# One broadcast for two factors in the feed-forward norm, and 64 more bytes ahead of V0 and V1

## The chip, the cores and the metric

The kernel runs on one core of a Trainium2 chip, in one launch. The time is the device time of one execution in microseconds (us). Beside the timed runs there is one profiled execution, from which all rows of the trace come. Engines are named as in the profile: PE is TensorE (PEld its weight loads), DVE is VectorE, ACT is ScalarE, POOL is GpSimd, SP issues the DMAs of the weights.

## What is computed

A sequence of 256 tokens of width 1024 goes through two layers of a first block and one layer of a second block, all in float32. A layer of the first block is

```
h = h + 0.5 * swiglu(rmsnorm(h, ffn1_norm), ffn1_wg, ffn1_wu, ffn1_wd)
h = h + hybrid_mixer(rmsnorm(h, mix_norm), ...)
h = h + 0.5 * swiglu(rmsnorm(h, ffn2_norm), ffn2_wg, ffn2_wu, ffn2_wd)
gate = sigmoid(rmsnorm(h, ple_norm) @ ple_w_gate);  h = h + gate * (p @ ple_w_proj)

swiglu(x, wg, wu, wd) = (silu(x @ wg) * (x @ wu)) @ wd          # 1024 -> 2816 -> 1024
```

`rmsnorm` divides each token by the root of its mean square plus 1e-6 and multiplies by a gain for each channel. The mixer projects the normed h, runs a short convolution branch and a state space branch (with a grouped norm and the product `m_w_out`, 2048 to 1024), gates and adds them and ends with `w_o`. The second block has a pooling and a convolution branch, and a feed-forward of squared relu, `w_up_2` (1024 to 4096) and `w_down_2`. So there are four gated feed-forwards, and their norm and their factor 0.5 are what the change touches.

## The kernel before, in words

**Layout.** Activations lie with channels on the 128 partitions and the 256 tokens along the free axis. A product with a weight matrix is cut into tiles of 128x128, 4948 in all, which SP loads in pieces of eight, in the order in which they are used. Each piece is split into two float32r parts (lines 319 to 333): ScalarE rounds it to `whi`, VectorE subtracts to `wlo`. The activations are split in the same way into a `hi` and a `lo` half. One tile is then three matmuls of 256 columns (`mm3`, lines 366 to 378): `whi` with hi, `whi` with lo, `wlo` with hi. The weight tile is the stationary operand, the activation the moving one. In the trace the operand's tile gives the name: `bank<-hs,whi` for instance is a product of the activations in hs0 or hs1.

**Where the activations lie.** hs0 and hs1 (lines 213 and 214, 16384 bytes in each partition) take turns as the operand of a stage that reads normed or raw h. The 22 blocks of a feed-forward's inner activations lie in V0 and V1, 11 in each (line 418); the mixer's 16 blocks of normed y lie there as well, as the operand of `m_w_out`. The mixer's merged branches lie in mg, the operand of `w_o`, at the place of the tile X. In the second block's feed-forward blocks 0 to 21 are in V0 and V1 and blocks 22 to 31 in V2, also at the place of X (line 1278). There the roles are exchanged (`mm3_rows`, lines 349 to 364): the activation is the stationary operand and 512 columns of weights the moving one, six matmuls for each of the 32 blocks, in two halves.

The allocator places the tiles one behind the other in the order of the code, with 32 bytes for a `small`. `more`, a tile of 192 bytes (line 516), comes behind X and ahead of ya, V0, V1, xd0 and xd1. In bytes from the start of a partition: weights' raw, whi and wlo tiles from 16512, each 4096 long; hs0 74048; hs1 90432; X (and mg and V2) 142912; more 167488; ya 167680; V0 175872; V1 198400; xd0 220928; xd1 (where p_sp lies) 225024.

**Order.** A small planner, `Flow` (lines 84 to 129), keeps an estimated clock for each engine while the program is written out: every stage is a generator that yields its estimated costs, and the order in which generators wake up is the order of the instructions on each engine. The order of the weight tiles is that of the main generator. [...]

**A feed-forward** (`ffn`, lines 541 to 588). Gate and up are 22 blocks each, with K of 8 tiles, from hs: 2 x 22 x 8 x 3 = 1056 matmuls. They start before the norm is known, since the norm's factor is one number for each token and can be multiplied in afterwards: hs holds h times the channel gains. The norm runs beside them (`norm`, lines 477 to 490): a column sum of the squares (two fp32 matmuls of 128 columns with a matrix of ones into the one PSUM bank `side`, `colsum`), the inverse root by Newton steps on VectorE (`rsqrt`), and then a broadcast (`bcast`, lines 468 to 475): the factors of 128 tokens stand one on each partition, and a matmul with the identity turns them into a row that is the same on all partitions, twice for 256 tokens. In the trace each fp32 matmul of these shows as two, so a broadcast is four rows `side<-ident,small`, and a column sum is four rows `side<-ones,acc`. ScalarE evicts the side bank into a row tile. The feed-forward wants the factor twice: `rb`, which multiplies the gate before its Silu, and `rhb`, half of it, which multiplies the result of the down product. Each gets a broadcast and an eviction of its own, the second with a scale of 0.5. In the first feed-forward of all there is no column sum, since its sums come from a copy of x with tokens on the partitions.

As soon as `rb` is there, each block is finished by `gate` (lines 549 to 560): a multiply on VectorE, Silu on ScalarE, a multiply, and the split into V. Down is 8 blocks with K of 22 tiles from V, 8 x 22 x 3 = 528 matmuls; the first two blocks are done side by side (`heads_of`), so that the last blocks of V have time to arrive.

**Other users of the broadcast.** The mixer's norm and the second block's norms ask for one row each; `norm_y` (lines 778 to 789) makes four broadcasts, one for each group of the grouped norm; the layer norm of the second block one.

Of the kernel before, what the change touches and what calls it, by code (L numbers as in the profile page):

```python
# [9 lines left out]
F32 = mybir.dt.float32  # L10
# [7 lines left out]
P = 128  # L18
T = 256
# [174 lines left out]
class Build:  # L194
# [270 lines left out]
            y = z  # L465
        self.roots.put(lock)

    def bcast(self, row, cols, scale=1.0):

        b = yield from self.side.get()  # L470
        for tt in range(2):
            w = self.mm(b[:, tt * P:(tt + 1) * P], cols[:, tt:tt + 1].to_broadcast([P, P]), self.ident, cost=0.213)
        yield w
        yield self.act(row, b[:, :T], scale=scale)
        self.side.put(b)

    def norm(self, s, rows, ev):

        c, y = self.small[8][:, :2], self.small[9][:, :2]
        yield s["ev"]  # L480
        self.chains += 1
        if "cols" in s:
            c = s["cols"]
        else:
            yield from self.colsum(s, EPS, D, c)
        yield from self.rsqrt(y, c)
        for row, scale in rows:
            yield from self.bcast(row, y, scale)
        self.fire(ev)
        self.chains -= 1  # L490

# [7 lines left out]
    def setup(self):  # L499
        nc = self.nc  # L500
        self.early = a = 32
        nc.sync.dma_start(self.vec[:, :a], self.vecd[:, :a])
        self.xev = [Event() for _ in range(ND)]
        self.flow.use("dma", 1.8)
        make_identity(nc, self.ident)
        nc.vector.memset(self.ones, 1.0)
        nc.vector.memset(self.shim, 0.0)

        nc.vector.memset(self.mask, 0.0)
        nc.gpsimd.affine_select(out=self.mask, in_=self.mask, pattern=[[1, P]], compare_op=ALU.is_ge,  # L510
                                fill=NEG, base=0, channel_multiplier=-1)
        self.chains = 0
        self.started = [Event() for _ in PIECES]
        extra = self.big.tile([P, 6, S * P], F32, name="extra", tag="X")
        self.extra = [extra[:, i, :] for i in range(6)]
        more = self.big.tile([P, 6, 8], F32, name="more", tag="more")
        self.small[18:] = [more[:, i, :] for i in range(6)]
        self.raws.free[:0] = self.extra
        for cv in self.cv.free:
            nc.vector.memset(cv[:, :16], 0.0)  # L520
        self.act(self.small[0], self.ones[:, :8], AF.Silu)
# [68 lines left out]
    def mixer(self, layer, sp, s, next_gain):  # L590
# [5 lines left out]
        rb = yield from self.rows.get()  # L596
# [38 lines left out]
        for n in range(ND):  # L635
            b = bs[1 + n] if n < 3 else (yield from self.unit("w_in", layer, GA + n, sp, ND))
# [141 lines left out]
        def norm_y(ys):  # L778
            for e in gsev:
                yield e  # L780
            yr = self.small[10]
            yield from self.rsqrt(yr, self.gsum)
            for g in range(4):
                gb = yield from self.rows.get()
                yield from self.bcast(gb, yr[:, 2 * g:2 * g + 2])
                row = Shared(self.rows, gb, 4)
                for j in range(4 * g, 4 * g + 4):
                    self.spawn(norm_block(ys, j, row))
                    yield 0.8

        def norm_block(ys, j, row):
            t = yield from self.vv.get()
            yield self.stt(t, xb[:, j, :], self.v("m_norm", layer, j), row.item, ALU.mult, ALU.mult)
            row.put()
            yield from self.split(ys, j, t)
            self.vv.put(t)
# [14 lines left out]
        for g in range(4):  # L811
# [4 lines left out]
            yield from heads(g)  # L816
        ys = Operand(*self.halves())
        self.spawn(norm_y(ys))

        sg = [self.big.tile([P, 4, T], F32, name="sg", tag=("xd0", "xd1")[i]) for i in range(2)]  # L820
# [10 lines left out]
        for n in range(ND):  # L831
            b = yield from self.unit("sc_w_out", layer, n, sc, ND)
            self.spawn(branch_a(n, b))
        for n in range(ND):
            b = yield from inp(GM + n)
# [18 lines left out]
        for n in range(ND):  # L854
            b = yield from self.unit("m_w_out", layer, n, ys, 16)
# [10 lines left out]
        for n in range(ND):  # L866
            b = bs[n] if n < 4 else (yield from self.unit("w_o", layer, n, mg, ND))
# [109 lines left out]
    def second(self, sp, ss):  # L977
# [9 lines left out]
        rb, r1b = (yield from self.rows.get()), (yield from self.rows.get())  # L987
# [3 lines left out]
        def norms():  # L991


            v1, v2, v12, r1, r12 = (x[:, :2] for x in self.small[12:17])
            yield from self.colsum(ss[0], EPS, D, v1)
            yield from self.colsum(ss[1], 0.0, D, v2)
            yield self.stt(v12, v1, EPS, v2)
            yield from self.rsqrt(r12, v12)
            yield from self.bcast(rb, r12)
            self.fire(rev)  # L1000
            for n in range(ND):
                yield from self.idle("dve")
                yield self.stt(xf[:, n, :], self.h[:, n, :], self.v("norm_mix_pre_2", None, n), rb, ALU.mult, ALU.mult)
                self.fire(xfo.ev[n])
            yield from self.rsqrt(r1, v1)
            yield from self.bcast(r1b, r1)
            yield 30.0
            for n in range(0, ND, 2):
                yield from self.idle("dve")
                yield self.mul(self.h[:, n:n + 2, :], self.h[:, n:n + 2, :], r1b.unsqueeze(1).to_broadcast([P, 2, T]))  # L1010
            self.rows.put(r1b)
            self.fire(hev)

        self.spawn(norms())

        def glu_part(n, ba, bg):
# [109 lines left out]
        for n in range(NSPLIT):  # L1126
            b = yield from self.unit(W, 0, 12 + n, sp, ND)
            self.spawn(gate(n, b))
        self.drop(sp)
        for n in range(NSPLIT, 2 * ND):  # L1130
            b = yield from self.unit(W, 0, 12 + n, xfo, ND)
# [6 lines left out]
        def layer_norm():  # L1138
            yield cvdone
            self.chains += 1  # L1140
            b = yield from self.banks.get()
            for n in range(4):
                w = self.mm(b[:, :T], self.ones, cacc[:, n, :], n == 0, n == 3, cost=0.43)
            yield w
            mu = yield from self.rows.get()
            yield self.act(mu, b[:, :T], scale=1.0 / 512)
            self.banks.put(b)
            yield self.sub(cacc, cacc, mu.unsqueeze(1).to_broadcast([P, 4, T]))
            self.rows.put(mu)
            p = yield from pr.get()  # L1150
            yield self.act(p, cacc, AF.Square)
            yield self.add(p[:, 0:2, :], p[:, 0:2, :], p[:, 2:4, :])
            s = yield from self.new_sum(0)
            yield self.add(s["acc"], p[:, 0, :], p[:, 1, :])
            pr.put(p)
            self.fire(s["ev"])
            c, rl = self.small[18][:, :2], self.small[19][:, :2]
            yield from self.colsum(s, EPS, 512, c)
            if sgev[-1].on:
                self.act(self.small[5], self.ones[:, :8], AF.Silu)  # L1160
            yield from self.rsqrt(rl, c)
            rlb = yield from self.rows.get()
            yield from self.bcast(rlb, rl)
            self.chains -= 1
            row = Shared(self.rows, rlb, 4)
            for n in range(4):
                self.spawn(ln_out(n, row))
                yield 0.4

        def ln_out(n, row):  # L1170
            t = yield from self.t.get()
            yield self.mul(t, cacc[:, n, :], row.item)
            row.put()
            yield self.act(t, t, AF.Silu, scale=self.v("conv_ln_g_2", None, n), bias=self.v("conv_ln_b_2", None, n))
            yield from self.split(pc, n, t)
            self.t.put(t)

        self.spawn(layer_norm())

        def mixed(n, b):  # L1180
# [3 lines left out]
        for n in range(4):  # L1184
            b = yield from self.banks.get()
# [11 lines left out]
        for n in range(ND):  # L1197
            b = yield from self.unit("w_pool_out_2", 0, n, px, 4)
# [13 lines left out]
        for n in range(ND):  # L1212
            b = yield from self.unit("w_conv_out_2", 0, n, pc, 4)
# [14 lines left out]
        for n in range(ND):  # L1228
            b = bs[n] if n < 4 else (yield from self.unit("w_o_2", 0, n, mg, ND))
            self.spawn(out(n, b))  # L1230
        self.drop(mg)
        rb = yield from self.rows.get()
# [16 lines left out]
        row = Shared(self.rows, rb, ND)  # L1249
# [29 lines left out]
        for j in range(NF2):  # L1279
            b = bs[j] if j < H else (yield from self.unit("w_up_2", 0, j, nsp, ND))  # L1280
# [6 lines left out]
        row = self.big.tile([P, D], F32, name="gain", tag="xd0")  # L1287
# [158 lines left out]
```

## Time and profile before

| what | value |
|---|---|
| timed runs | 1841.87, 1833.98, 1841.28 us; median 1841.28 |
| profiled execution | 1848.41 us, its span 1846.6 us |
| mean granted TensorE clock | 0.995 |
| matmuls | 14916 |
| DVE, ACT, POOL busy | 1316.8, 1050.3, 10.5 us |
| weights from HBM | 340.31 MB read, 185 GB/s over the span |

How to read the rows below: a group's row gives line, engine, operation, output<-inputs, shape, count, then busy time and the mean duration of one, then the engine's idle time before them. A window's row gives the stretch in us from the span's start, its length, the busy time and count of TensorE, the granted clock, the share of DMA time and GB/s. A row of the timeline begins with its start and length in us. [...]

### The profile page before, as it was taken

Reading aid. Unit: us, or ns where it says so; the run is one execution under the profiler, and the core shown is the slowest. Engines: PE = TensorE matmul, PEld = TensorE weight load, DVE = VectorE, ACT = ScalarE, POOL = GpSimd, SP = SyncE. Lnnn points to the kernel's source line nnn. Section 1 sums busy time; section 2 is a strip of 40 time slices with the busy share of each in tenths; the row PEclk is TensorE's granted clock in tenths of the full one; section 3 lists DMA queues with packets and bytes.
Section 4 is the critical chain, followed back from the end, with each engine's and each line's share of the span. In section 5 each row is a group of like instructions: output and inputs, shape, how many; then the busy total and the mean of one; then the engine's idle time right before and its main releaser. Section 6 shows DMA issues by size and latency. Waiting matters only on the chain.

```text
span 1846.6 us, 36550 instructions
## 1 busy us (share of the span) xinstructions
PE 1817.4 (98%) x14916; PEld 1776.4 (96%) x14916; DVE 1316.8 (71%) x2236; ACT 1050.3 (57%) x1707; POOL 10.5 (1%) x22
## 2 busy tenths in 40 slices
PE   8999999999999999999999999999999999989997
PEld 8999999999999999999999999999999999889986
DVE  6666789888576656866578988766665689877643
ACT  5554678665454444644457966555544468656542
POOL 0000000000000000000000000000000000000000
PEclk9999999999999999999999999999999999989999
DMA  7666576655656665665557666465666653546552
GB/s 253 204 195 186 161 252 194 220 180 158 203 169 196 184 186 179 187 187 186 183 169 255 186 199 191 157 204 189 190 189 184 184 181 126 175 149 204 184 192 76
DMA packets 92696, 343.83 MB, mean 186 GB/s; under 512 B 10448, under 2 KB 10960, under 8 KB 91376
## 3 DMA queue, kind: packets, MB, share of 16 engines
q1 hardware_dynamic: 90720, 327.25, 57.1%
q0 software_dynamic: 1520, 13.73, 2.0%
q8 instruction: 116, 1.90, 0.4%
q10 hardware_dynamic: 288, 0.52, 0.1%
q14 instruction: 52, 0.43, 0.1%
HBM read 340.31 MB, written 1.15 MB: 185 GB/s over the span
## 4 chain that ended last, share of the span: by engine, by line
PE 92%; DVE 3%; ACT 2%; DMA 2%; issue 1%; SPq 0%; DVEq 0%; ACTq 0%
PE bank L237 90%; DMA raw<-in_w 1%; PE side L237 1%; DVE wlo L244 1%; ACT L266 1%; ACT whi L266 1%; PE bank L733 0%; DMA h<-in_x 0%; ACT dec L266 0%; DVE small L257 0%; DVE cv L257 0%; DVE hs L257 0%; DVE acc L244 0%; DVE t L244 0%; DVE vv L257 0%
## 5 line engine op out<-in xcount | busy, mean ns | idle before, releaser
L237 PE MATMUL bank<-hs,whi 128*128 128x256 f32 x6928 | 1224.7, 281 | 12.0 <-ACT whi L266 7.5
L237 PEld LDWEIGHTS bank<-hs,whi 128*128 128x128 f32 x6928 | 1058.0, 189 | 19.2 <-ACT whi L266 7.8
L244 DVE TENSOR_TENSOR wlo<-raw,whi 128x1024 fp32r<-128x1024 f32 (+1 forms) x602 | 732.2, 1219 | 397.7 <-ACT whi L266 396.9
L266 ACT ACTIVATE whi<-raw 128x1024 fp32r<-128x1024 f32 (+1 forms) x602 | 634.5, 1057 | 660.1 <-issue 343.4
L237 PE MATMUL bank<-hs,wlo 128*128 128x256 f32 x3464 | 968.9, 280 | 1.0 <-DVE wlo L244 1.0
L237 PEld LDWEIGHTS bank<-hs,wlo 128*128 128x128 f32 x3464 | 656.6, 190 | 1.8 <-DVE wlo L244 1.7
L237 PE MATMUL bank<-V,whi 128*128 128x256 f32 x1920 | 342.7, 282 | 0.0
L237 PEld LDWEIGHTS bank<-V,whi 128*128 128x128 f32 x1920 | 295.3, 188 | 0.0
L237 PE MATMUL bank<-V,wlo 128*128 128x256 f32 x960 | 270.8, 282 | 0.0
L237 PEld LDWEIGHTS bank<-V,wlo 128*128 128x128 f32 x960 | 180.8, 188 | 0.0
L237 PE MATMUL bank<-whi,V 128*128 128x512 f32 x256 | 80.3, 393 | 0.0
L244 DVE TENSOR_TENSOR t<-bank,row 128x256 f32<-128x256 f32 x159 | 64.2, 416 | 19.4 <-PE bank L237 12.5
L257 DVE SCALAR_TENSOR_TENSOR cv<-bank,vec,cv 128x253 f32<-128x253 f32 (+2 forms) x144 | 63.4, 472 | 2.9 <-ACT cv L266 2.5
L244 DVE TENSOR_TENSOR vv<-bank,t 128x256 f32<-128x256 f32 x152 | 62.5, 417 | 3.1 <-ACT t L266 2.9
L244 DVE TENSOR_TENSOR V<-vv,V 128x256 fp32r<-128x256 f32 x152 | 62.2, 418 | 1.5 <-ACT V L266 1.3
L266 ACT ACTIVATE V<-vv 128x256 fp32r<-128x256 f32 x152 | 59.9, 402 | 2.6 <-DVE vv L257 1.6
L237 PEld LDWEIGHTS bank<-whi,V 128*128 128x128 f32 x256 | 48.2, 188 | 11.1
L237 PE MATMUL bank<-wlo,V 128*128 128x512 f32 x128 | 50.5, 394 | 0.0
L266 ACT ACTIVATE dec<-dec,tb 128x256 f32<-128x256 f32 (+1 forms) x128 | 49.5, 444 | 0.1
L244 DVE TENSOR_TENSOR acc<-acc,sq 128x256 f32<-128x256 f32 x101 | 42.3, 419 | 8.8 <-ACT sq L266 8.2
L266 ACT ACT_TABLE_LOAD x37 | 47.5, 1283 | 1.3 <-PEq L1441 0.7
L237 PE MATMUL bank<-mg,whi 128*128 128x256 f32 x256 | 45.3, 281 | 0.0
(152 smaller groups left out, 1114.7 us busy)
## 6 DMA issues: line engine op xcount, KB each, us to landing
raw<-in_w SPq DMA_DIRECT2D x613, 512.0 KB, 4.3
dec<-cum_d POOLq DMA_DIRECT2D x8, 1536.0 KB, 10.1
extra<-in_w SPq DMA_DIRECT2D x4, 512.0 KB, 8.3
xt<-in_xt SPq DMA_DIRECT2D x1, 1024.0 KB, 11.3
h<-in_x SPq DMA_DIRECT2D x1, 512.0 KB, 8.2
praw<-in_p POOLq DMA_DIRECT2D x2, 256.0 KB, 4.6
gain<-in_row POOLq DMA_DIRECT2D x1, 512.0 KB, 4.8
out<-o SPq DMA_DIRECT2D x2, 256.0 KB, 2.7
```

The costliest lines, as they stand in the source:

```text
L237: self.nc.tensor.matmul(ps, w, x, start=start, stop=stop, **k)
L244: self.nc.vector.tensor_tensor(out, a, b, op=op)
L257: self.nc.vector.scalar_tensor_tensor(out, a, s, b, op0=op0, op1=op1)
L266: self.nc.scalar.activation(out=out, in_=a, func=func, **k)
```

## The change

`bcast` takes a list of rows with their scales. It broadcasts once and evicts the side bank into each of the rows, one eviction behind the other, and gives the bank back after the last. `norm` hands it both rows of the feed-forward at once, so that the second broadcast of each of the four feed-forwards is gone and both evictions read the same bank. The other callers hand over a list of one.

`more` grows from 6 x 8 to 8 x 8 numbers, from 192 to 256 bytes in each partition. The two added entries are not used. Everything behind it lies 64 bytes higher: ya 167744, V0 175936, V1 198464, xd0 220992, xd1 225088. V0 and V1 then start 64 bytes past a multiple of 256, as hs0 does.

```diff
-    def bcast(self, row, cols, scale=1.0):
+    def bcast(self, rows, cols):
 
         b = yield from self.side.get()
         for tt in range(2):
             w = self.mm(b[:, tt * P:(tt + 1) * P], cols[:, tt:tt + 1].to_broadcast([P, P]), self.ident, cost=0.213)
         yield w
-        yield self.act(row, b[:, :T], scale=scale)
+        for row, scale in rows:
+            wait = self.act(row, b[:, :T], scale=scale)
+        yield wait
         self.side.put(b)
...
         yield from self.rsqrt(y, c)
-        for row, scale in rows:
-            yield from self.bcast(row, y, scale)
+        yield from self.bcast(rows, y)
         self.fire(ev)
...
-        more = self.big.tile([P, 6, 8], F32, name="more", tag="more")
+        more = self.big.tile([P, 8, 8], F32, name="more", tag="more")
         self.small[18:] = [more[:, i, :] for i in range(6)]
...
-                yield from self.bcast(gb, yr[:, 2 * g:2 * g + 2])
+                yield from self.bcast([(gb, 1.0)], yr[:, 2 * g:2 * g + 2])
```

More of the change, by code (lines that the diff above doesn't have):

```diff
@@ L998, in norms @@
             yield from self.rsqrt(r12, v12)
-            yield from self.bcast(rb, r12)
+            yield from self.bcast([(rb, 1.0)], r12)
             self.fire(rev)
@@ L1005, in norms @@
             yield from self.rsqrt(r1, v1)
-            yield from self.bcast(r1b, r1)
+            yield from self.bcast([(r1b, 1.0)], r1)
             yield 30.0
@@ L1162, in layer_norm @@
             rlb = yield from self.rows.get()
-            yield from self.bcast(rlb, rl)
+            yield from self.bcast([(rlb, 1.0)], rl)
             self.chains -= 1
```

## The prediction

> **What bounds the kernel now.** I read the page first, for the engine that sets the end, then the groups of matmuls by operand, then windows of TensorE by stage, and at last the order of TensorE's instructions where the feed-forward norm cuts into it.
>
> ```profile
> PE 1817.4 (98%) x14916; PEld 1776.4 (96%) x14916; DVE 1316.8 (71%) x2236; ACT 1050.3 (57%) x1707; POOL 10.5 (1%) x22
> PE 92%; DVE 3%; ACT 2%; DMA 2%; issue 1%; SPq 0%; DVEq 0%; ACTq 0%
> L237 PE MATMUL bank<-V,whi 128*128 128x256 f32 x1920 | 342.7, 282 | 0.0
> L237 PE MATMUL bank<-V,wlo 128*128 128x256 f32 x960 | 270.8, 282 | 0.0
> L237 PE MATMUL bank<-whi,V 128*128 128x512 f32 x256 | 80.3, 393 | 0.0
> ```
>
> TensorE is busy for 98% of the span, and 92% of the chain that ended last is TensorE. The V groups waited for nothing (0.0). So the time is the number of matmuls times the distance from one start to the next, and a change moves the time if it moves that distance. The duration of one (282 ns) is no help: it overlaps its neighbours. The distance comes from windows laid inside one stage: length plus one matmul (0.28 us), divided by the count, since a matmul that only reaches into the window is counted too.
>
> ```profile
> core 0: us, PE busy (x), PEclk, DMA share, GB/s
> 31.40:133.90 102.50, 102.50 (x907) 1.00 0.67 201
> 135.00:195.00 60.00, 60.00 (x508) 1.00 0.64 185
> 197.50:204.50 7.00, 7.00 (x64) 1.00 0.66 199
> 438.90:442.60 3.70, 3.70 (x35) 1.00 0.57 167
> 443.40:447.60 4.20, 4.20 (x38) 1.00 0.29 110
> 453.00:469.00 16.00, 16.00 (x143) 1.00 0.69 221
> 470.00:514.00 44.00, 44.00 (x373) 1.00 0.62 194
> 515.00:536.00 21.00, 21.00 (x180) 1.00 0.50 156
> 537.50:542.80 5.30, 5.30 (x47) 1.00 0.85 294
> 548.80:662.90 114.10, 114.10 (x971) 1.00 0.62 189
> 664.00:725.00 61.00, 61.00 (x516) 1.00 0.63 188
> 768.90:880.20 111.30, 111.30 (x947) 1.00 0.62 190
> 881.00:943.00 62.00, 62.00 (x519) 1.00 0.60 186
> 1297.00:1410.00 113.00, 113.00 (x962) 1.00 0.64 191
> 1412.00:1473.00 61.00, 61.00 (x517) 1.00 0.62 187
> 1745.00:1774.00 29.00, 29.00 (x126) 1.00 0.56 182
> 1776.00:1787.00 11.00, 11.00 (x50) 1.00 0.60 192
> ```
>
> By stage, in ns: gate and up of the first feed-forward (31.4) 113.3; its down, from V, 118.7; the mixer's last product from hs (453) 113.8; m_w_out, from V, (470) 118.7; w_o, from mg, (515) 118.2; gate and up of the second feed-forward (548.8) 117.8, its down 118.8; of the third (768.9) 117.8, its down 120.0; of the fourth 117.8 and 118.5. The granted clock is 1.00 in every row and TensorE has no idle time, so neither clock nor waiting makes the difference. There are three paces. The same tiles hs0 and hs1 run at **A**, 113.3, or **B**, 117.8, for a whole stage; V never runs at either, but at **C**, 118.7 to 120.0.
>
> What goes with C is the place. In the allocation of the kernel before, hs0 and hs1 start 64 bytes past a multiple of 256 in each partition (74048, 90432), mg and V2 too (142912), the weights 128 past one, V0 and V1 0 past one (175872, 198400). The last stage shows the same with V as stationary operand: over V0 and V1 (1745) 233 ns a matmul with the 393 ns of its row for the edge, over V2 (1776) 228.
>
> What chooses A or B is the break. The norm's fp32 broadcasts cut into the stream, and after each the pace can be another:
>
> ```profile
> 28.38 0.28 PE L237 MATMUL bank<-hs,wlo 128*128 128x256 f32 x1
> 28.72 0.28 PE L237 MATMUL bank<-hs,wlo 128*128 128x256 f32 x1
> 28.84 0.60 PE L237 MATMUL side<-ident,small 128*128 128x128 f32 x4
> 29.52 0.28 PE L237 MATMUL bank<-hs,wlo 128*128 128x256 f32 x1
> 29.87 0.28 PE L237 MATMUL bank<-hs,wlo 128*128 128x256 f32 x1
> 30.58 0.28 PE L237 MATMUL bank<-hs,wlo 128*128 128x256 f32 x1
> 30.69 0.61 PE L237 MATMUL side<-ident,small 128*128 128x128 f32 x4
> 31.38 0.28 PE L237 MATMUL bank<-hs,wlo 128*128 128x256 f32 x1
> 31.72 0.28 PE L237 MATMUL bank<-hs,wlo 128*128 128x256 f32 x1
> ...
> 546.84 0.28 PE L237 MATMUL bank<-hs,wlo 128*128 128x256 f32 x1
> 546.96 0.61 PE L237 MATMUL side<-ident,small 128*128 128x128 f32 x4
> 547.32 0.49 PE L237 MATMUL bank<-hs,whi 128*128 128x256 f32 x2
> 547.65 0.28 PE L237 MATMUL bank<-hs,wlo 128*128 128x256 f32 x1
> 547.99 0.28 PE L237 MATMUL bank<-hs,wlo 128*128 128x256 f32 x1
> 548.10 0.65 PE L237 MATMUL side<-ident,small 128*128 128x128 f32 x4
> ```
>
> Three matmuls lie between two wlo starts: 0.34 us is A, 0.35 to 0.36 is B. In the first feed-forward the stream is at A, the first broadcast puts it at B, the second back at A, and there it stays for 907. In the second it comes at B (537.5: 118.7, short), the first broadcast puts it at A (547.65 to 547.99: 0.34), the second at B, and there it stays for 971. The mixer's breaks alternate too: 35 in 3.7 us are A (B would give 34), 38 in 4.2 us are B (A would give 39).
>
> **The change, part by part.** *The second broadcast goes*, once in each of four feed-forwards. From 28.72 to 29.52 are 0.80 us where 0.34 would be without the break: 0.46 each, four times, all on TensorE's path: **-1.8**. The second eviction stays as an instruction and comes right behind the first:
>
> ```profile
> L266 ACT ACTIVATE row<-side x24: 366/385/387, 29.5 to 1648.4; 128x256 f32<-128x256 f32 x24
> ```
>
> Its 0.385 us lie beside the first gate multiply on VectorE, which needs only the first row; behind it on ScalarE is that gate's Silu, which waits for the multiply anyway. Without that cover it costs 4 x 0.39 = 1.5 us, of ScalarE, not TensorE. The side bank comes free one eviction later, and its next user is a whole stage away. No wait is added, and no DMA or queue is passed.
>
> *The pace after the norm turns over.* This is worth more than the instructions. In the first feed-forward, the pace after the first broadcast is now kept: 907 matmuls at B for A, 907 x 4.5 ns = **+4.0**. In the second, third and fourth the row before the removed break is at A (shown for the second; the third and fourth end at B like it, and I take them alike): 971, 947 and some 971 at A for B: -4.3, -4.2, -4.3 = **-12.8**.
>
> *V0 and V1 move 64 bytes*, to hs0's place in 256. The trace has no V there; the nearest rows are hs, between 113.3 and 117.8, and V itself as it is, up to 120.0. I take what the stage before it runs at, since mg goes on into hs at one pace without a break (515 and 537.5). From the code, down has 8 x 22 x 3 = 528 matmuls, m_w_out 8 x 16 x 3 = 384, w_o 192. First down, after B: 528 x 0.9 = **-0.5**, and the first 69 of the mixer behind it, now at A (197.5: 113.8), +**0.3**. Both m_w_out follow A: 768 x 5.3 = **-4.1**. Behind them w_o and the 48 heads of the next gate keep A for B: 480 x 4.4 = **-2.1**. The other downs: 2 x 528 x 5.3 = -5.6, and from 120.0 528 x 6.6 = -3.5: **-9.1**. In the last stage 2 x 22 x 6 = 264 matmuls are nearer V2's pace: 5 ns by the windows, of which I trust 4, **-1.0**. p_sp, 96 matmuls, moves as V does: between 0 and -0.5, taken **-0.3**. Elementwise operands that shift along count nothing: their engines are at 71% and 57%.
>
> The sum: -1.8 + 4.0 - 12.8 - 0.5 + 0.3 - 4.1 - 2.1 - 9.1 - 1.0 - 0.3 = **-27.4 us**. The profiled execution took 1848.41 (span 1846.6), so 1821.0. The runs shown, 1833.98 to 1841.87, lie 6.5 to 14.4 below it, spread by 7.9. I read that as the same choice of pace: the second break comes five matmuls after the first and waits for the eviction (0.65 for 0.61), so its outcome can differ between runs, at 4.3 us a feed-forward. The changed kernel has no such break; so I take off only 1 us: **1820**.
>
> Do the feeding engines keep up with A everywhere? The first gate stage ran at A over 102 us with 201 GB/s and no wait, so I expect no new bound.
>
> [...]
>
> **The rivals.** *The first feed-forward stays at A* (the start, with its waits, leaves the stream so that one break ends at A): -4.0, -0.3, and its down gains 2.8 for 0.5: 1821.0 - 6.6 = 1814. For it: the start differs from every other stage. Against: the rows at 28.72 to 30.58 are B. *The later gates stay at B*, only V gains: 1821.0 + 12.8 = 1834. For it: all three end at B now. Against: 547.65 to 547.99. *The place does nothing*, and the paces stay as they are: 1848.4 - 1.8 = 1846.6, which beside the runs is no change. For it: C could belong to the work beside it, such as the down stage's evictions. Against: m_w_out has other work beside it and the same 118.7. [...] *Slower: B is carried on.* Once the first feed-forward ends at B and V no longer interrupts it, B runs into the mixer and through its breaks. It decides at the first break after 204.5. +4.0, V at B for C 2880 x 0.9 and 0.7 more for the 120.0 stage (-3.3), -1.8, -1.0, and the mixers' hs products, 2 x 1920 by the code and about half at A now: 1920 x 4.4 = +8.4, all of them +16.9. That is +6.3 to +14.8, 1855 to 1863, 1859 in the middle. Against: both mixer rows (438.9, 443.4) show breaks that turn B to A.
>
> **How the numbers follow.** The forecast has 0.50, the first feed-forward at A 0.17, later gates at B 0.12, no effect of place 0.15, B carried on 0.06. About 0.5%, 9 us, is what can be told from no change: against a median of 1841, faster is below 1832. The first two cases are, and most of the third against the profiled time: 0.78; same 0.16; slower 0.06. The range goes down to 1808 (the second case less the 6 us by which runs lie under the profile) and up to 1836 (the third, with the mixers' breaks 2 us either way).
>
> **What would show it.** Windows over the changed trace: first gates near 117.8, the other three near 113.3; downs at 113 to 118, none at 118.7; w_o at 113.3; the last stage even over its 32 steps. One broadcast before each gate stage with two evictions behind it. V at 118.7 again makes the place wrong; gates at 117.8 make the break wrong; TensorE waits in the gates would mean that the feeding engines don't keep up.

## The result and the profile after

The changed kernel takes 1820.8 us (median of four, 1818.1 to 1822.13), the kernel before 1841.57 beside it (1833.98 to 1847.4): a ratio of 0.9888, 95% interval 0.9849 to 0.9926. The profiled execution took 1822.13, its span 1820.3, which is 26.3 us less than the span before. The medians differ by less, 20.8, since the profiled execution before (1848.41) lies above all the timed runs beside it; what differs between executions of that kernel is shown further down (e9, e10). The forecast was 1820, from a sum of -27.4.

TensorE is as busy as before:

```profile
PE 1789.6 (98%) x14900; PEld 1749.2 (96%) x14900; DVE 1318.0 (72%) x2236; ACT 1050.9 (58%) x1707; POOL 10.5 (1%) x22
```

The windows of TensorE in the changed kernel, by stage (stretch, length, busy time and count, clock, DMA share, GB/s), read as before: length plus 0.28 us, over the count.

```profile
31.00:138.00 107.00, 107.00 (x911) 1.00 0.63 192
140.00:200.00 60.00, 60.00 (x512) 1.00 0.62 188
201.00:208.50 7.50, 7.50 (x66) 1.00 0.57 201
213.00:255.00 42.00, 42.00 (x359) 1.00 0.54 169
...
475.00:517.00 42.00, 42.00 (x373) 1.00 0.63 205
518.50:539.00 20.50, 20.50 (x184) 1.00 0.57 167
...
550.00:660.00 110.00, 110.00 (x973) 1.00 0.66 197
661.00:719.50 58.50, 58.50 (x518) 1.00 0.65 195
762.50:869.50 107.00, 107.00 (x946) 1.00 0.64 197
870.50:929.00 58.50, 58.50 (x518) 1.00 0.65 196
984.00:1009.00 25.00, 25.00 (x223) 1.00 0.81 294
1279.00:1388.00 109.00, 109.00 (x964) 1.00 0.67 199
1389.50:1448.00 58.50, 58.50 (x519) 1.00 0.66 196
1642.00:1718.00 76.00, 76.00 (x648) 1.00 0.59 195
1719.00:1748.00 29.00, 29.00 (x128) 1.00 0.57 187
1751.00:1762.00 11.00, 11.00 (x50) 1.00 0.58 192
```

The first gate stage (31) is at 117.8 ns, pace B, where it had been at A. Its down, from V (140), is at 117.7, and so are the mixer's first products from hs (201: 117.9). From there on V runs at A: m_w_out (475) 113.4, w_o behind it (518.5) 112.9 within the count's edges, the three other gate stages (550, 762.5, 1279) 113.3 to 113.4, their downs (661, 870.5, 1389.5) 113.3 to 113.5. No row is at 118.7 any more. In the last stage V (1719, with 0.39 us for the edge) is at 229.6, V2 (1751) at 227.8; one matmul more or less in so short a window moves these by 2 and by 5 ns. The starts say it more closely: V's 132 matmuls of the first half run from 1718.69 to 1748.93, 229.1 each, where before they ran from 1744.09 to 1774.74, 232.2 each. TensorE is busy in every one of these windows, so the gain is in the distance between starts, not in waits.

The order of TensorE where the norm cuts into the first gates (start, length):

```profile
29.64 0.28 PE L237 MATMUL bank<-hs,wlo 128*128 128x256 f32 x1
29.75 0.60 PE L237 MATMUL side<-ident,small 128*128 128x128 f32 x4
30.11 0.48 PE L237 MATMUL bank<-hs,whi 128*128 128x256 f32 x2
30.43 0.28 PE L237 MATMUL bank<-hs,wlo 128*128 128x256 f32 x1
30.55 0.40 PE L237 MATMUL bank<-hs,whi 128*128 128x256 f32 x2
30.78 0.28 PE L237 MATMUL bank<-hs,wlo 128*128 128x256 f32 x1
```

There is one broadcast. Behind it three matmuls take 0.35 us (B), and no second break turns the pace back: the window from 31 on is what that leaves.

ScalarE and VectorE at this broadcast:

```profile
30.39 0.66 ACT L266 ACTIVATE row<-side 128x256 f32<-128x256 f32 x2 [5.97 <-PE side L237]
...
30.81 1.09 DVE L244 TENSOR_TENSOR t<-bank,row 128x256 f32<-128x256 f32 x3 [3.82 <-ACT row L266]
```

Both evictions run as a pair, 0.66 us together, and the gate's multiply starts 0.42 us after the first of them began, while the second still runs: it is covered.

### The profile page after: what moved, and what is told of

The parts are those of the page before. It is cut to its first block, busy times and chain, and to the rows that moved or that the text cites. A ratio compares the mean times of both kernels' runs of the same rounds, so it can differ in the third digit from the quotient of the medians.

```text
span 1820.3 us, 36518 instructions
## 1 busy us (share of the span) xinstructions
PE 1789.6 (98%) x14900; PEld 1749.2 (96%) x14900; DVE 1318.0 (72%) x2236; ACT 1050.9 (58%) x1707; POOL 10.5 (1%) x22
## 4 chain that ended last, share of the span: by engine, by line
PE 91%; DVE 4%; ACT 2%; DMA 2%; issue 1%; SPq 0%; DVEq 0%; ACTq 0%
PE bank L237 90%; DMA raw<-in_w 1%; DVE wlo L244 1%; PE side L237 1%; ACT L266 1%; ACT whi L266 0%; PE bank L734 0%; DMA h<-in_x 0%; DVE cv L257 0%; DVE small L257 0%; DVE hs L257 0%; DVE acc L244 0%; DVE t L244 0%; DVE vv L257 0%; DVE hs L244 0%
## 5 line engine op out<-in xcount | busy, mean ns | idle before, releaser
L237 PE MATMUL bank<-V,whi 128*128 128x256 f32 x1920 | 329.0, 277 | 0.0
L237 PEld LDWEIGHTS bank<-V,whi 128*128 128x128 f32 x1920 | 290.4, 188 | 0.0
L237 PE MATMUL bank<-V,wlo 128*128 128x256 f32 x960 | 265.8, 277 | 0.0
L266 ACT ACTIVATE hs<-h,vec 128x256 fp32r<-128x256 f32 x80 | 38.4, 498 | 11.9 <-DMA h<-in_x 7.1
```

Source lines behind the costliest of these rows:

```text
L237: self.nc.tensor.matmul(ps, w, x, start=start, stop=stop, **k)
L266: self.nc.scalar.activation(out=out, in_=a, func=func, **k)
```

## The experiments

A and B are the two paces of the prediction, 113.3 and 117.8 ns; a break is a pair of fp32 matmuls (four rows) that cuts into the stream.

**The two parts apart.** The first run has the single broadcast and leaves `more` as it was; the second has the longer `more` and leaves both broadcasts.

```diff
# e1: the changed kernel, with
-        more = self.big.tile([P, 8, 8], F32, name="more", tag="more")
+        more = self.big.tile([P, 6, 8], F32, name="more", tag="more")
# e2: the kernel before, with
-        more = self.big.tile([P, 6, 8], F32, name="more", tag="more")
+        more = self.big.tile([P, 8, 8], F32, name="more", tag="more")
```

> The change's first part alone: one broadcast with two evictions, more at 192 bytes, so V0 and V1 stay at 0 in 256. Theory (the place sets V's pace, the breaks choose between the paces A, 113.3 ns, and B, 117.8 ns): V stays at 118.7 to 120 in all six of its stages, the first gate stage goes to B (+4.0 us), the other three to A (-12.8), four breaks of 0.46 go (-1.8): 10 to 11 us under the profiled 1848.4, so about 1838. Rival 'breaks alone': the place is worth nothing and this is as fast as the whole change, 1821. Rival 'place alone': gates keep their paces, only the breaks' own time goes, 1846.6.

> The change's second part alone: two broadcasts as before, more at 256 bytes, so V0 and V1 at 64 in 256. Theory: V follows the stage ahead of it: first down at A (528 x 5.4 ns = -2.8 us), both m_w_out at A (-4.1), w_o and the heads behind at A (-2.1), the other gates still end at B after their second break, their downs at B (-0.5, -1.2, -0.5), last stage -1.0: some 12 us under 1848.4, about 1836. Rival 'breaks alone': as before, 1841 to 1848. Rival 'place alone': as the whole change, 1821.

e1 took 1837.52 (1836.99 to 1838.4), e2 1836.78 (1831.51 to 1848.13 in ten runs); the kernel before, on the same chip, 1848.56 (1837.85 to 1854.1 in 14). The ratios are 0.994 (0.992 to 0.996) and 0.9946 (0.9926 to 0.9965). Windows of e1 (first gates and down, m_w_out, second gates):

```profile
30.00:137.00 107.00, 107.00 (x910) 1.00 0.64 194
138.50:200.00 61.50, 61.50 (x515) 1.00 0.61 186
...
474.00:518.00 44.00, 44.00 (x373) 1.00 0.66 196
...
552.50:662.00 109.50, 109.50 (x968) 1.00 0.65 197
```

and of e2 (first gates and down, second gates and down):

```profile
33.00:134.50 101.50, 101.50 (x898) 1.00 0.68 203
136.00:194.50 58.50, 58.50 (x519) 1.00 0.63 195
...
545.00:658.00 113.00, 113.00 (x962) 1.00 0.61 189
659.00:720.00 61.00, 61.00 (x520) 1.00 0.64 189
```

In e1 the gates are turned over (117.9, then 113.4) and V stays between 118.5 and 120.0: m_w_out is at 118.7 as before, and the first down, now behind gates at B, at 120.0, where it was at 118.7. In e2 the gates stay as before (113.3, then 117.8) and V takes the pace ahead of it (113.3, 117.8). Each part does its own thing, neither alone is worth the whole, and both rivals fall. The two ratios multiply to 0.9886, where the whole change has 0.9888. That they agree so closely is partly luck, since the kernel before stood at 1848.56 beside these two and at 1841.57 beside the whole change.

**Which places are good.** V at 128 and at 192 in 256, by `more` of 320 and 384 bytes:

```diff
# e3, e4: the changed kernel, with
-        more = self.big.tile([P, 8, 8], F32, name="more", tag="more")
+        more = self.big.tile([P, 10, 8], F32, name="more", tag="more")     # e4: [P, 12, 8]
```

> The changed kernel with more at 320 bytes: V0 and V1 at 128 in 256, where the weights' tiles start too. Theory (what counts is the place in 256 against the weights): V is at neither A nor B but at 118 ns or more, as at 0 or worse, so the time is the changed kernel's 1820.8 plus 2880 x 3 to 6 ns: 1830 to 1838. Rival (only the old place 0 is bad): V at A or B and 1821.

> The changed kernel with more at 384 bytes: V0 and V1 at 192 in 256, so at hs0's place in 128 but not in 256. If the place in 128 is what counts: V at A or B as in the changed kernel, 1821. If the place in 256 counts: another pace for V, 118 ns or more, 1830 or above.

e3 took 1836.8 and e4 1835.58, a single execution each. Of e3 the first down and the last stage over V, of e4 the third down and the last stage:

```profile
139.00:201.00 62.00, 62.00 (x519) 1.00 0.62 185
...
1735.00:1763.00 28.00, 28.00 (x125) 1.00 0.55 187
```

```profile
875.00:936.00 61.00, 61.00 (x520) 1.00 0.64 190
1732.00:1760.00 28.00, 28.00 (x122) 1.00 0.58 188
```

At 128, the weights' own place, V runs at 120.0. At 192 it runs at 117.8 though the gates ahead of it were at A. So the place in 256 counts, not that in 128, and of the four places only 64 lets V have A. Where V is the stationary operand the order is another: 227.1 at 128 and 232.7 at 192 by these windows, and by the starts of its first 132 matmuls 226.7 ns at 128 (from 1733.92 to 1763.84) and 233.3 at 192 (from 1730.47 to 1761.27), beside the 232.2 at 0 and 229.1 at 64 of above.

**The place or the tile.** Two runs move hs instead of V, and everything together:

```diff
# e5: the changed kernel with more at [P, 6, 8], and
-        self.small = [fix(f"small{i}", [P, 8]) for i in range(6)]
+        self.small = [fix(f"small{i}", [P, 8 if i < 5 else 56])[:, :8] for i in range(6)]
# e6: the changed kernel with
+        fix("pad", [P, 16])
         self.raws = ring("raw", NR, [P, S * P])
```

> The changed kernel with small5 160 bytes longer and more back at 192 bytes: hs0, hs1 and mg move to 0 in 256 (V's place before the change), V0 and V1 to 192, the weights stay at 128. Theory (the place in 256 against the weights sets the pace, for any tile): hs and mg now run at 118.7 to 120, wherever they ran at 113.3 or 117.8. About 7900 of their matmuls were at A and 2900 at B: 7900 x 5.4 + 2900 x 0.9 + 2880 of V x 4.5 = 58 us more than 1821, so about 1879, up to 1893 at 120. Rival (V was slow for what runs beside its stages, not for its place): hs keeps 113.3 and 117.8, and the time stays between 1821 and 1836.

> The changed kernel with a pad of 64 bytes ahead of every tile: the weights at 192 in 256, hs, mg, V at 128; nothing moves against anything else. Theory 'relation' (what counts is the operand's place against the weights'): 1821, the same paces. Theory 'absolute' (V at 128 ran at 120 in e3 for the 128 itself): hs, mg and V all at 120, some 70 us more.

In e5 small5 is 192 bytes longer, not the 160 of the expectation; the places are as it names them. It took 1875.47, a little under the 1879 to 1893 expected. Its second gates, from hs at 0:

```profile
561.00:676.00 115.00, 115.00 (x972) 1.00 0.62 188
```

That is 118.6, V's old pace, and neither A nor B. That the down stage's other work made V slow is ruled out. e6 took 1823.73; its second gates and down:

```profile
550.00:660.00 110.00, 110.00 (x973) 1.00 0.65 196
661.00:719.50 58.50, 58.50 (x519) 1.00 0.64 194
```

113.3 and 113.3 with V at 128 and the weights at 192. In e3 V at 128 with the weights at 128 had 120.0. So it is the place against the weights that counts. There is a rival, since TensorE's loads are not all that touches the weights' tiles: ScalarE and VectorE write whi and wlo at the same place. The trace of the kernel before speaks against it. In its first down, the 105 triples of matmuls that lie wholly beside such a write have a mean distance of 118.65, the 20 that lie beside none 118.67; in its third down it is 120.0 for 86 of the one and 22 of the other.

**Another distance from the weights.** hs, mg and V all at 96, 32 below the weights:

```diff
-        self.small = [fix(f"small{i}", [P, 8]) for i in range(6)]
+        self.small = [fix(f"small{i}", [P, 8 if i < 5 else 16])[:, :8] for i in range(6)]
```

> The changed kernel with small5 32 bytes longer: hs, mg, V all at 96 in 256, 32 below the weights. Theory (64 below the weights is the best of the places, since 128 below and the same place are slower): hs, mg and V at 114 to 120, 1821 to 1890. Rival (any place that differs from the weights' and from 128 below them does): A and B again, 1821.

It took 1870.71, with one pace for gates and downs alike, here the second gates, and a later stretch:

```profile
560.00:674.00 114.00, 114.00 (x966) 1.00 0.64 189
...
1632.00:1660.00 28.00, 28.00 (x236) 1.00 0.68 219
```

118.3, and 119.8 in the later stretch. Nothing here comes near 113.3, and no place tried beats 64 below the weights.

**Breaks as a tool.** If a break turns the pace, the one stage that the change made worse can be turned back, and another that was at B in the profiles of both kernels, w_up (117.9 before, 117.7 after), can be turned too.

```diff
# e7: the changed kernel, with
-        yield from self.bcast(rows, y)
+        for part in ([[r] for r in rows] if "cols" in s else [rows]):
+            yield from self.bcast(part, y)
# e8: e7, and in norm2, behind self.fire(r2ev):
+            b = yield from self.side.get()
+            for tt in range(2):
+                w = self.mm(b[:, tt * P:(tt + 1) * P], y[:, tt:tt + 1].to_broadcast([P, P]), self.ident, cost=0.213)
+            yield w
+            self.side.put(b)
```

> The changed kernel, but the first feed-forward of all makes two broadcasts again, as before the change; the other three make one. Theory (a break turns the pace over): the first gates go back to A after the second break (-4.0 us), their down follows at A (528 x 4.4 = -2.3), the mixer's first 69 (-0.3) and, one break later, its 362 (-1.6), and one break costs 0.46: 1820.8 - 7.8 = 1813. Rival (the first stage is at B for another reason, such as the start's waits): 1821.3.

> As e7, and in the second block's feed-forward, after its inverse root, one broadcast that nobody reads, as a break alone (it stands for no part of the result): w_up's stage ran at B (659 matmuls at 117.8) after the column sum. Theory: the break puts it at A, 650 x 4.4 = -2.9 + 0.46: 2.4 us under e7, about 1811. Rival (a broadcast gives only its own cost): 0.46 over e7.

e7 took 1814.91 (1811.81 to 1817.48), ratio to the kernel before 0.9875 (0.9849 to 0.9902); e8 1811.63 (1809.83 to 1814.7), ratio 0.9859 (0.9837 to 0.9881). The kernel before stood at 1837.33 there. Of e7 the first gates, their down, and w_up; of e8 the stream ahead of the column sum, between it and the added break, and behind the break:

```profile
32.00:133.50 101.50, 101.50 (x898) 1.00 0.65 203
135.00:193.50 58.50, 58.50 (x518) 1.00 0.63 196
...
1636.50:1710.00 73.50, 73.50 (x651) 1.00 0.60 201
```

```profile
1625.00:1633.00 8.00, 8.00 (x73) 1.00 0.21 66
1635.00:1644.50 9.50, 9.50 (x83) 1.00 0.55 170
1646.00:1709.00 63.00, 63.00 (x558) 1.00 0.65 201
```

The first gates and their down are back at 113.3 and 113.5. In e8 the pace goes 113.4, 117.8, 113.4: a broadcast that nobody reads turns the stage. But in e7's profile w_up was at 113.3 by itself, where the changed kernel's is at 117.7; the stream before it starts again after a pause (from 1623.26 to 1625.19 in the changed kernel), and w_up differs between executions of one program too (117.8 in e9, 113.3 in e10). So the 3.3 us between e7 and e8, whose runs overlap, are not all shown to be the break's. e8 has the lowest times found, and its runs don't overlap with those of the changed kernel (1818.1 to 1822.13). But the kernel before stood 4.2 us lower beside e7 and e8 than beside the changed kernel, and the intervals of the ratios overlap. So that e8 is faster than the changed kernel rests on the paces of its stages, not on the times.

**Where the spread of the kernel before comes from.** The kernel before twice more, as it is, and e2 with its second broadcast later, when the side bank has long been free:

> The kernel before once more, for a second profile beside its time. Theory (the spread of its runs, 1834 to 1854, is the choice of pace after the second broadcast, which waits for the first eviction): a run far from 1848 has one to three of the later gate stages at A instead of B, 4.3 us each. Rival (the spread has another source): all three gates at B again and the time differs by other stages or by waits.

> The kernel before a third time, as e9: theory, times and gate paces differ together by steps of 4.3 us; rival, they don't.

```diff
# e11: e2, with (in norm)
-        for row, scale in rows:
-            yield from self.bcast(row, y, scale)
+        yield from self.bcast(rows[0][0], y, rows[0][1])
         self.fire(ev)
+        for row, scale in rows[1:]:
+            yield 3.0
+            yield from self.bcast(row, y, scale)
```

> As e2 (place alone, two broadcasts), but the second broadcast comes 3 us of planned time after the first, so that it no longer waits for the eviction of the side bank. Theory (the wait is the source of the spread): the later gates go A after the first and, some 25 matmuls on, B after the second break in every run, so about e2's 1836 with runs within 4 us of each other. Rival (the spread lies elsewhere): the runs spread over 10 us or more, as e2's did (1831.5 to 1848.1).

e9 took 1841.46, e10 1838.53. The second, third and fourth gates and w_up of e9, then w_up of e10, whose gates are as e9's:

```profile
550.50:659.50 109.00, 109.00 (x964) 1.00 0.63 197
766.00:877.00 111.00, 111.00 (x945) 1.00 0.63 190
1294.00:1403.50 109.50, 109.50 (x969) 1.00 0.65 198
1660.00:1736.50 76.50, 76.50 (x652) 1.00 0.59 196
```

```profile
1660.00:1733.50 73.50, 73.50 (x651) 1.00 0.62 201
```

The same program has its second and fourth gates at 113.4 and 113.3 here, and at 117.8 in the profile shown first. That is 2 x 4.3 = 8.6 us for the 7 between 1848.4 and 1841.5; the other stages together take 1.6 us more in e9. Between e9 and e10 w_up goes from 117.8 to 113.3, 650 x 4.5 = 2.9 us, which is the whole difference of their times. e11 took 1838.47 (1834.75 to 1840.51 in ten runs): 5.8 us of spread against e2's 16.6, and its later gates are all at 117.8. Its ratio to the kernel before beside it (1841.21) is only 0.9988 (0.9976 to 1.0): the kernel before had two later gates at A in both profiles taken there (e9, e10), e11 none. So the wait of the second break is most likely a source of the spread (ten runs each of e2 and e11, not taken side by side), more than the 4 us expected remain, and runs above what three gates at B give (1854.1 for the kernel before, 1848.13 for e2) are not explained.

## Why the prediction was right, point by point

**The bound and the paces** held: TensorE is busy for 98% after the change too, and the time went with the distance between starts. But V had two paces of its own, 118.7 and 120.0, which the prediction took for one.

**The place.** V took the pace of the stage ahead of it, as mg had: first down 117.7 for the predicted B, the other five V stages at 113.3 to 113.5 for A. The -0.5, -4.1, -2.1 and -9.1 stand; e5 and e6 show that it is the place against the weights, which the prediction had left open by naming hs's place only. With V at 128, weights at 192 give 113.3 (e6) and weights at 128 give 120.0 (e3). What in TensorE makes the difference, no run shows.

**The breaks.** +4.0 for the first gates and -12.8 for the others came as worked out (31: 117.8; 550, 762.5 and 1279: A). That was the bolder term, since the third and fourth gates' short stretch at A was taken on the second's word. The trace of the kernel before has it, 0.34 us between these starts of the third, and the same from 1295.71 to 1296.05 in the fourth:

```profile
767.73 0.28 PE L237 MATMUL bank<-hs,wlo 128*128 128x256 f32 x1
...
768.07 0.28 PE L237 MATMUL bank<-hs,wlo 128*128 128x256 f32 x1
```

But a break does not turn the pace every time, and that the mixer's breaks alternate, as the prediction says, is not so for the last of its four broadcasts. In the kernel before it comes at 452.36, and the stream is at A ahead of it (113.3 by the row below) and behind it (453: 113.8):

```profile
448.40:452.20 3.80, 3.80 (x36) 1.00 0.35 134
```

In the changed kernel it comes at 457.60. The 33 matmuls ahead of it, counted from the start at 453.75 to that at 457.49, are at 113.3, and behind it the row below gives 113.5:

```profile
458.50:474.00 15.50, 15.50 (x139) 1.00 0.71 222
```

No number of the sum rests on that broadcast; but which breaks turn the pace was read off, not derived.

**Sizes that were off.** The last stage: by its starts V went from 232.2 to 229.1, 3.1 ns where I trusted 4, so -0.8 for -1.0. The mixer of the first layer: I had +0.3 for its first 69 matmuls, but the two breaks behind them, coming from B, left the next 362 at B too (213: 117.8). In the kernel before that stretch was at A, by its window 113.5:

```profile
208.60:249.40 40.80, 40.80 (x362) 1.00 0.57 172
```

362 x 4.4 = +1.6, which the sum lacks. That is the parity of breaks that I applied to the gates and didn't carry on into the mixer. In the second layer's mixer the row at 984 is at 113.4. I had said nothing of this stretch, which was at B before (117.6):

```profile
998.00:1033.00 35.00, 35.00 (x300) 1.00 0.81 274
```

For its 312 matmuls that is about -1.3. So the mixers' two surprises nearly cancel, and that the sum came so close is in this part luck. What is left of the 1.1 us between the sum's 27.4 and the spans' 26.3 is about the start: the first broadcast comes at 29.75, for 28.84 before, 0.9 us later, ahead of anything that the change touches.

**The offset to the runs.** The reading of the spread as a choice of pace is shown for the second and fourth gates and for w_up, not for the slowest runs. Taking off 1 us was near enough: the changed kernel's profiled execution lies 1.3 us above the median of its runs. With two of the later gates at A, as e9 and e10 have them, the kernel before takes about 1840 and not 1848, so such executions already have part of the -12.8, which fits the 20.8 us between the medians.

**The rivals.** That the first feed-forward stays at A didn't come, but e7 shows its price: 1814.9 for the 1814 worked out, with the first gates and their down at A. In its profiled execution w_up was at A as well, some 2.9 us that do not belong to this rival, so the match of the totals is partly luck. That the place does nothing falls by e2 and e5. That B is carried on through the mixer came for one stretch of 362 and ended at the next break, as the rows against it had said.

## What to carry to other kernels

Where one engine is busy all the time, measure the distance between starts by stage; two stages of the same instruction with different distances (here 113.3 and 118.7 ns) can hide a gain that no wait or idle row shows. Then compare where their operands start, here modulo 256 bytes and against the other operand, before anything is rewritten. And a small instruction that cuts into a steady stream can cost far more, or far less, than its own time (here the second broadcast, 0.46 us by itself, saved 4.0 us in the first gates, 907 matmuls at 113.3 that are at 117.8 without it, and cost 4.3 us in the second, 971 at 117.8 that are at 113.3 without it): look at the pace behind it, for as long as it lasts.

## What the runs showed of the hardware that was not expected

The distance of a 256-column float32r matmul with a weight load for each, by where the moving operand starts against the weights, modulo 256 bytes: 128 below 118.7 or 120.0, 64 below 113.3 or 117.8, 32 below 118.3 (119.8 in one stretch), the same place 120.0, 64 above 117.8. At 64 below, an fp32 pair in between could turn one pace into the other (113.3 to 117.8 at 29.75 in the changed kernel) and sometimes did not (113.3 on both sides at 457.60), while hundreds of matmuls, a change of the tile or of the bank did not turn it: in the changed kernel's second feed-forward 973 matmuls from hs, 24 to a bank, ran at 113.3 and the 518 from V behind them at 113.5. With 512 columns of weights moving and the activations stationary, the same place was best: by the starts 226.7, then 64 below 229.1, 128 below 232.2, 64 above 233.3. Why a stream keeps its pace, why a break turns it or not, and what it is about the place that counts, none of these runs shows.
